# Three quarters of a feed-forward's first product recast in Strassen's form, on an already tuned hybrid block

## The chip, the cores and the metric

One core of a Trainium2 chip runs the whole kernel. The metric is the device time of one execution in microseconds; three executions of the kernel before gave 858.98, 860.34 and 860.87 us, median 860.34 us. One more execution was profiled.

The engines spoken of here are TensorE (PE in the profile, its weight loads PEld), VectorE (DVE), ScalarE (ACT), GpSimd (POOL) and SyncE (SP), which issues most of the DMAs.

## The reference

One layer on 512 frames of 1024 channels. Three gated branches (linear attention, forgetting attention, attention into a memory) are merged and added to the residual; then comes a feed-forward, and a last norm:

```python
u2 = rmsnorm(h, g_ffn[l])
h = h + jnp.square(jax.nn.relu(u2 @ w_ff1[l])) @ w_ff2[l]
return rmsnorm(h, g_final)
```

`w_ff1` is 1024 x 4096 and `w_ff2` 4096 x 1024. The change touches these two products and the last norm. Their inputs and outputs stay float32.

## The kernel before

Every large matmul works on split operands: a float32 block is cast on ScalarE to a high part (fp32r), VectorE subtracts that from the block and so writes the low part, and `mm3` (line 121) issues three matmuls, high by high, high by low, low by high. A weight block is 128 x 1024 (512 KB): SyncE loads it into one of three `raw` tiles of pool `wp`, and its two parts go into one of three `hi`/`lo` pairs. PE's order is written by hand; the order of the other engines' queues comes from a scheduler that runs when the program is built, and each queue is then worked off strictly in that order.

The feed-forward runs in four quarters of 1024 hidden channels (loop at line 1002). In each quarter:

- **First product** (`gT`, line 126): eight blocks of `w_ff1`. One block is eight weight tiles of 128 x 128, each taken by `mm3` against all 512 frames of `u2h`/`u2l`: 24 matmuls with 512 columns. `act_evac` (line 899) applies relu and square on ScalarE and builds seven left factors with VectorE, split into `ch`/`cl`.
- **Second product** (`second`, line 968): Strassen's seven products in Winograd's form, in the order 1, 2, 5, 6, 7, 4, 3. Each takes two weight blocks `i = 0, 1`, twelve 512-column matmuls a block. The right factors 5, 6, 7, 4 are sums of blocks that are formed in place by DMAs of GpSimd that add a second block to the one in SBUF (line 979). `split_b` (line 889) has the three `hi`/`lo` pairs and a fourth of its own (`bhi`/`blo`). Products 1 and 5 stay in PSUM over all quarters (`held`), 6 and 7 are summed in `R6`, `R7`, the others are added to the residual `hN`.

In the last quarter the sums of products 1, 5 and 6 (`E`, `G`) are added to `hN` by six DMAs of GpSimd (line 950), product 7 by VectorE, and `finish` (line 918) norms a row tile as soon as its last half is there and sends both halves out. The first of all tiles, `first`, are computed in halves of 256 frames (`half`, line 855) while the norm of the last frames still runs; `u2_turn` (line 843) transposes the normed frames on PE and splits them into `u2h`/`u2l`.

Below, `c1` to `c14` are the fourteen weight blocks of one second product in PE's order; all fourteen take twelve 512-column matmuls each. `F1` to `F14` are those of the first product in the new form.

Of the kernel before, what the change touches and what calls it, by code (L numbers as in the profile page):

```python
# [17 lines left out]
P = 128  # L18
# [14 lines left out]
def chunk_list():  # L33

    L = []
    L += [("T", "w_mem_kv", P * j) for j in range(4)]
    L += [("N", "w_mem_kv", 2 * j, 512) for j in range(4)]
    L += [("G",)]
    L += [("T", "w_in", OFF["fq"]), ("T", "w_in", OFF["fk"])]
    L += [("N", "w_in", 2 * j, OFF["fv"]) for j in range(4)]  # L40
    for j in range(1, 4):
        L += [("T", "w_in", OFF["fq"] + P * j), ("T", "w_in", OFF["fk"] + P * j)]
    for n, c in (("gk", 2), ("gq", 2)):
        L += [("T", "w_in", OFF[n] + P * j) for j in range(c)]
    L += [("N", "w_in", 2 * j, OFF["gv"]) for j in range(4)]
    for n, c in (("gg", 4), ("mq", 4)):
        L += [("T", "w_in", OFF[n] + P * j) for j in range(c)]
    for g, o in (("gate_fox", "w_fox_o"), ("gate_mem", "w_mem_o"), ("gate_gla", "w_gla_o")):
        for j in range(KT):
            L.append(("T", "w_in", OFF[g] + P * j))  # L50
            if j % 2 == 0:
                L.append(("O", o, j // 2))
    for c in range(2):
        L += [("N", "w_out", 2 * j, 512 * c) for j in range(4)]
    for q in range(4):
        L += [("T", "w_ff1", P * (8 * q + j)) for j in range(8)]
        L += [("B", q, i, b) for b in ("11", "21", "12", "22") for i in range(2)]
    return L
# [3 lines left out]
def hybrid_block(ctx, tc, chunks, wst, xT, memT, xN, cols, gffn, gfin, wup, cst, out):  # L62
# [41 lines left out]

    def load_w(key, eng=None):
        i = index[key]
        raw = wp.tile([P, 1024], F32, tag="raw", name=nm("raw"))
        (eng or nc.sync).dma_start(raw, wst[i])
        return raw

    def split_w(raw):
        hi = wp.tile([P, 1024], F32R, tag="hi", name=nm("whi"))
        lo = wp.tile([P, 1024], F32R, tag="lo", name=nm("wlo"))
        nc.scalar.copy(hi, raw)  # L114
        nc.vector.tensor_tensor(lo, raw, f(hi), op=ALU.subtract)  # L115
        return hi, lo
# [690 lines left out]
    u2h = up.tile([P, KT, S], F32R, tag="uhi", name="u2h")  # L807
    u2l = up.tile([P, KT, S], F32R, tag="ulo", name="u2l")
    with pool("outp") as op_:
# [4 lines left out]
        run(branch("gate_gla", "w_gla_o", ogh, ogl, 2, last=(mh, ml)))  # L814

# [28 lines left out]
        def u2_turn(t):  # L844
            for g in range(2):
# [3 lines left out]
                sl = slice(t * P, (t + 1) * P)  # L849
                last = split(u2h[:, 4 * g:4 * g + 4, sl], u2l[:, 4 * g:4 * g + 4, sl], pt)  # L850
# [4 lines left out]
        def half(j, i, ks=range(KT)):  # L855
            sl = slice(256 * i, 256 * i + 256)
            for k in ks:
                mm3(first[j][:, sl], ws[j][0][:, k, :], ws[j][1][:, k, :], u2h[:, k, sl], u2l[:, k, sl], k == 0, k == KT - 1)
# [12 lines left out]
    mst.close()  # L871
# [7 lines left out]

    with pool("ff") as yp:  # L880
        R6, R7 = ([yp.tile([P, 512], F32, name=f"R{n}{t}") for t in range(2)] for n in (6, 7))
        NQ = 4
        held = {}
        split_n = [0]

        def scratch():
            return yp.tile([P, S], F32, tag="sq", name=nm("sq"), bufs=3)

        def split_b(raw):
            split_n[0] += 1  # L890
# [4 lines left out]
            return [t.rearrange("p (k c) -> p k c", k=2) for t in (hi, lo)]  # L895

        A = []

        def act_evac(ps):

            sq = scratch()
            nc.scalar.activation(sq, ps, AF.Relu)
            nc.scalar.activation(sq, sq, AF.Square)
            if not A or A[-1][2] is not None:
                h, l = (yp.tile([P, 7, 256], F32R, tag=g, name=nm(g), bufs=4) for g in ("ch", "cl"))
                split(h[:, 0, :], l[:, 0, :], sq[:, :256])
                A.append([h, l, None, sq])
                return
            h, l, _, sa = A[-1]
            A[-1][2] = sq  # L910
            split(h[:, 1:3, :], l[:, 1:3, :], sq.rearrange("p (a t) -> p a t", a=2))
            ss = yp.tile([P, 4, 256], F32, tag="ss", name=nm("ss"))
            a11, a21, a12, a22 = sa[:, :256], sa[:, 256:], sq[:, :256], sq[:, 256:]
            for o, x, y in ((0, a21, a22), (2, a11, a21), (1, a11, ss[:, 0, :]), (3, a12, ss[:, 1, :])):
                nc.vector.tensor_tensor(ss[:, o, :], x, y, op=ALU.subtract)
            split(h[:, 3:7, :], l[:, 3:7, :], ss)

        def finish(t, c, n):
            sumsq(scratch(), hN[t], t, c, n)
            if n == 1:  # L920
                r = rms_tile(yp, t)
                for g, eng in ((0, nc.scalar), (1, nc.sync)):
                    gs_ = slice(512 * g, 512 * g + 512)
                    nc.vector.scalar_tensor_tensor(hN[t][:, gs_], hN[t][:, gs_], r, gl[:, gs_], op0=ALU.mult, op1=ALU.mult)
                    eng.dma_start(out[t * P:(t + 1) * P, gs_], hN[t][:, gs_])
# [4 lines left out]
        def add(to, x, op=ALU.add):  # L930
            nc.vector.tensor_tensor(to, to, x, op=op)

        def evac(q, n, t, ps):
            last = q == NQ - 1
            if n == 1 and last:
                add(C(0, 0, t), ps)
            if n in (6, 7):
# [5 lines left out]
            if n == 6 and last:  # L943
                if t == 0:
                    held["G"] = yp.tile([P, 2, 512], F32, tag="ss", name=nm("G"))
                E, G = R6[t], held["G"][:, t, :]
                nc.vector.tensor_tensor(E, held[1][t], R6[t], op=ALU.subtract)
                nc.vector.tensor_tensor(G, held[5][t], E, op=ALU.subtract)
                for to, x in ((C(1, 0, t), E), (C(1, 1, t), G), (C(0, 1, t), G)):
                    nc.gpsimd.dma_start(to, x, accum_op=ALU.add)  # L950
            if n == 7 and last:
                add(C(1, 1, t), R7[t], ALU.subtract)
                finish(2 + t, 1, 0)
                add(C(1, 0, t), R7[t])
# [4 lines left out]
            if n == 3:  # L959
                add(C(0, 1, t), ps)  # L960
                if last:
                    finish(t, 1, 1)
            if n == 2:
                add(C(0, 0, t), ps)
                if last:
                    finish(t, 0, 0)

        def second(q):
            raw = {(b, i): yp.tile([P, 1024], F32, tag=f"b{b}{i}", name=nm("raw")) for b in ("11", "21", "12", "22")
                   for i in range(2)}  # L970
            for (b, i), t in raw.items():
                nc.sync.dma_start(t, wst[index["B", q, i, b]])

            def factor(n, i):

                to, x = {1: ("11", None), 5: ("11", "12"), 6: ("11", "22"), 7: ("12", "22"), 4: ("11", "21"), 3: ("22", None),
                         2: ("21", None)}[n]
                if x is not None:
                    nc.gpsimd.dma_start(raw[to, i], wst[index["B", q, i, x]], accum_op=ALU.add)  # L979
                return split_b(raw[to, i])  # L980

            for n, slot in ((1, 0), (2, 1), (5, 3), (6, 4), (7, 5), (4, 2), (3, 6)):
# [5 lines left out]
                end = q == NQ - 1 and n == 3  # L988
                steps = [[0, 1]] if end else [[0], [1]]
                for js in steps:  # L990
                    w = {i: factor(n, i) for i in js}
                    for t in range(2):
                        for i in js:
                            for k in range(2):
                                p = 2 * i + k
                                sl = slice(t * P, (t + 1) * P)
                                mm3(ps[t], A[p][0][:, slot, sl], A[p][1][:, slot, sl], w[i][0][:, k, :], w[i][1][:, k, :],
                                    p == 0 and not (keep and q), p == 3 and (not keep or q == NQ - 1))
# [3 lines left out]
        for q in range(NQ):  # L1002
            A.clear()
            for j in range(8):
                if q == 0 and j < 2:
                    act_evac(first[j])
                    continue
                key = ("T", "w_ff1", P * (8 * q + j))
                if q == 0 and j < 4:
                    with tc.issue_after(norm_end):  # L1010
                        w = get_w(key)
                else:
                    w = get_w(key)
                run(gT(w, u2h, u2l, act_evac))
# [3 lines left out]
            second(q)  # L1018


def layout(inputs):
# [7 lines left out]
    for i, c in enumerate(chunks):  # L1029
# [4 lines left out]
        elif c[0] == "B":  # L1034
# [3 lines left out]
            for n in range(2):  # L1038
                wst[i, :, 512 * n:512 * n + 512] = W["w_ff2"][(j + 2 * n) * P:(j + 2 * n + 1) * P, cs]
        elif c[0] == "O":  # L1040
# [61 lines left out]
```

## Time and profile before

| | us |
|---|---|
| median of three executions | 860.34 |
| the profiled execution, whole | 859.26 |
| its span, first to last instruction of the program | 857.1 |
| TensorE busy | 840.5 |
| VectorE busy | 498.4 |
| ScalarE busy | 404.3 |
| GpSimd busy | 87.4 |
| stage before the feed-forward tiles (start of `half`) | 0 to 520.2 |
| feed-forward, to the last matmul | 520.2 to 848.3 |

The profile counts a matmul as busy from its start to a modelled end. Matmuls overlap in the array, so what one costs on PE is read from the distance of two starts in the timeline, not from its duration. The same holds, in small, for VectorE and ScalarE: a row that merges several instructions shows their time together.

### The profile page before, as it was taken

Reading aid. Unit: us, or ns where it says so; the run is one execution under the profiler, and the core shown is the slowest. Engines: PE = TensorE matmul, PEld = TensorE weight load, DVE = VectorE, ACT = ScalarE, POOL = GpSimd, SP = SyncE. Lnnn points to the kernel's source line nnn. Section 1 sums busy time; section 2 is a strip of 40 time slices with the busy share of each in tenths; the row PEclk is TensorE's granted clock in tenths of the full one; section 3 lists DMA queues with packets and bytes.
Section 4 is the critical chain, followed back from the end, with each engine's and each line's share of the span. In section 5 each row is a group of like instructions: output and inputs, shape, how many; then the busy total and the mean of one; then the engine's idle time right before and its main releaser. Section 6 shows DMA issues by size and latency. Waiting matters only on the chain.

```text
span 857.1 us, 10630 instructions
## 1 busy us (share of the span) xinstructions
PE 840.5 (98%) x4041; PEld 695.4 (81%) x4041; DVE 498.4 (58%) x832; ACT 404.3 (47%) x646; POOL 87.4 (10%) x96
## 2 busy tenths in 40 slices
PE   8899999999999999999999999999999999999995
PEld 5778788888888888787888889888888888888884
DVE  5775657766444556574533546665556645665577
ACT  8764747754332431322332434655455345535642
POOL 5100000000000011211112100011001000110022
PEclk9999999999999999999999999999999999999998
DMA  8433232322222122124222413969435933791156
GB/s 319 151 123 125 106 115 99 123 75 75 76 96 99 53 96 75 50 74 172 99 98 99 172 50 124 318 122 238 155 97 122 273 123 83 149 281 53 26 102 168
DMA packets 32146, 108.28 MB, mean 126 GB/s; under 512 B 3872, under 2 KB 4832, under 8 KB 32096
## 3 DMA queue, kind: packets, MB, share of 16 engines
q1 hardware_dynamic: 24832, 84.00, 27.3%
q0 software_dynamic: 5472, 18.35, 12.2%
q10 hardware_dynamic: 1792, 5.26, 1.8%
q8 instruction: 32, 0.52, 0.2%
q14 instruction: 18, 0.15, 0.1%
HBM read 103.90 MB, written 2.13 MB: 124 GB/s over the span
## 4 chain that ended last, share of the span: by engine, by line
PE 90%; ACT 3%; DVE 3%; DMA 1%; issue 1%; POOL 0%; SPq 0%; DVEq 0%; POOLq 0%; ACTq 0%
PE mm L122 25%; PE mm L123 24%; PE mm L124 24%; PE a L123 3%; PE a L124 3%; PE a L122 3%; PE a L739 1%; DMA h<-G 1%; PE a L756 1%; PE a L499 1%; PE a L498 1%; PE a L750 1%; DMA memr<-in_memT_dram 1%; PE a L467 1%; PE a L466 1%
## 5 line engine op out<-in xcount | busy, mean ns | idle before, releaser
L115 DVE TENSOR_TENSOR wlo<-raw,whi 128x1024 fp32r<-128x1024 f32 x103 | 129.9, 1264 | 133.4 <-ACT whi L114 131.7
L114 ACT CAST whi<-raw 128x1024 fp32r<-128x1024 f32 x103 | 108.4, 1053 | 168.6 <-PE mm L123 128.4
L122 PE MATMUL mm<-uhi,whi 128*128 128x512 f32 x352 | 139.7, 397 | 0.0
L124 PE MATMUL mm<-uhi,wlo 128*128 128x512 f32 x352 | 137.6, 391 | 0.0
L123 PE MATMUL mm<-ulo,whi 128*128 128x512 f32 x352 | 137.5, 391 | 0.0
L122 PE MATMUL mm<-u2h,whi 128*128 128x512 f32 x240 | 93.4, 389 | 0.0
L123 PE MATMUL mm<-u2l,whi 128*128 128x512 f32 x240 | 93.4, 389 | 0.0
L124 PE MATMUL mm<-u2h,wlo 128*128 128x512 f32 x240 | 93.4, 389 | 0.0
L175 DVE TENSOR_TENSOR lo<-raw,hi 128x1024 fp32r<-128x1024 f32 x42 | 51.2, 1224 | 49.6 <-ACT hi L174 49.1
L124 PEld LDWEIGHTS mm<-uhi,wlo 128*128 128x128 f32 x352 | 66.2, 188 | 14.2
L122 PEld LDWEIGHTS mm<-uhi,whi 128*128 128x128 f32 x352 | 66.4, 189 | 13.5 <-issue 0.7
L123 PEld LDWEIGHTS mm<-ulo,whi 128*128 128x128 f32 x352 | 66.3, 188 | 12.9
L174 ACT CAST hi<-raw 128x1024 fp32r<-128x1024 f32 x42 | 44.0, 1053 | 62.5 <-PE mm L123 23.5
L979 POOL DMA_DIRECT2D raw<-in_wst_dram x32 | 28.1, 877 | 277.2 <-DVE lo L175 208.0
L123 PEld LDWEIGHTS mm<-u2l,whi 128*128 128x128 f32 x240 | 45.0, 188 | 9.4
L122 PEld LDWEIGHTS mm<-u2h,whi 128*128 128x128 f32 x240 | 45.0, 188 | 9.3
L124 PEld LDWEIGHTS mm<-u2h,wlo 128*128 128x128 f32 x240 | 45.0, 188 | 9.3
L122 PE MATMUL mm<-hi,ch 128*128 128x512 f32 x120 | 46.7, 389 | 0.0
L123 PE MATMUL mm<-lo,ch 128*128 128x512 f32 x120 | 46.7, 389 | 0.0
L124 PE MATMUL mm<-hi,cl 128*128 128x512 f32 x120 | 46.7, 389 | 0.0
L590 POOL TENSOR_TENSOR acc<-acc,th 128x512 f32<-128x512 f32 x16 | 24.0, 1503 | 102.7 <-DVE th L589 102.7
L668 POOL MEMSET qpos<- 64x512 f32 x2 | 1.0, 524 | 268.6 <-PE mm L124 268.6
(320 smaller groups left out, 1641.1 us busy)
## 6 DMA issues: line engine op xcount, KB each, us to landing
raw<-in_wst_dram SPq DMA_DIRECT2D x144, 512.0 KB
raw<-in_wst_dram POOLq DMA_DIRECT2D x32, 512.0 KB, 5.3
nFb<-dF ACTq DMA_DIRECT2D x8, 512.0 KB
xr<-in_xT_dram SPq DMA_DIRECT2D x4, 512.0 KB
h<-in_xN_dram SPq DMA_DIRECT2D x4, 512.0 KB
memr<-in_memT_dram SPq DMA_DIRECT2D x4, 256.0 KB
h<-G POOLq DMA_DIRECT2D x4, 256.0 KB, 5.7
out_dram<-h ACTq DMA_DIRECT2D x4, 256.0 KB
```

The source lines that it names most:

```text
L114: nc.scalar.copy(hi, raw)
L115: nc.vector.tensor_tensor(lo, raw, f(hi), op=ALU.subtract)
L122: nc.tensor.matmul(ps, lh, rh, start=start, stop=False)
L123: nc.tensor.matmul(ps, lh, rl, start=False, stop=False)
L124: nc.tensor.matmul(ps, ll, rh, start=False, stop=stop)
L174: nc.scalar.copy(hi, src)
L175: return nc.vector.tensor_tensor(lo, src, f(hi), op=ALU.subtract).ins
L466: nc.tensor.matmul(ps[:, :w], q, K[e][:, 0, :w], start=True, stop=False)
L467: nc.tensor.matmul(ps[:, :w], q, K[e][:, 1, :w], start=False, stop=True)
L498: nc.tensor.matmul(po[:, q0:], vv, PTh[:, c0:c0 + w], start=n == 0, stop=False)
L590: nc.gpsimd.tensor_tensor(acc[j], acc[j], th, op=ALU.add)
L979: nc.gpsimd.dma_start(raw[to, i], wst[index["B", q, i, x]], accum_op=ALU.add)
```

## The change

- **Quarters 2 to 4 of the first product** become Strassen products too (`first_product`). `u2` is kept in four slots of 4 x 256 columns (two halves of the channels by two halves of the frames), with three more slots for sums of them (`u2s`), made on VectorE after the first quarter's fourth tile (`u2_sums`), and one slot overwritten by a sum when the first quarter's tiles are done (`u2_last`). Each half quarter is seven products, in the order 1, 2, 5, 6, 3, 7, 4; each takes one weight block as eight weight tiles against 256 columns. So the weight blocks of a quarter's first product go from 8 to 14, and the matmuls from 192 of 512 columns to 336 of 256. The results are combined by VectorE (`first_evac`).
- **Four of the seven right factors** there are sums of blocks of `w_ff1`. They are made during the earlier stages in DRAM: 24 DMAs of GpSimd, 1 MB each, half of them plain copies and half adding (`next_sum`), each waiting for the cast of every second weight block from the ninth on, and most for an earlier one of the chain to land.
- **The second product** runs 1, 2, 5, 3, 6, 7, 4. Its left factors are now made in three slots of `ch`/`cl` that are rewritten while it runs, and a fourth. Its blocks `11` and `12` go to four tiles of their own (`b11`, `b12`; till `u2_sums` they hold an unsplit copy of `u2`, which `u2_turn` writes with eight more copies on ScalarE), `21` and `22` through the ring of `raw` tiles, which has four now. The fourth `hi`/`lo` pair is gone.
- **The last quarter's corrections** are done by VectorE and the six DMAs are gone. `finish` multiplies the first half by the final gain early; at the end VectorE scales one half of a row tile and ScalarE the other.

```diff
+    tsum = {(n, q): dram.tile([2, P, 1024], F32, name=f"T{n}_{q}") for q in range(1, 4) for n in (1, 2, 3, 4)}
+    def sum_ops():
+        for q in range(1, 4):
+            for n, src, add in ((1, "11", 0), (3, "12", 0), (1, "12", 1), (3, "22", 1), (2, 1, 0), (2, "22", 1), (4, 2, 0),
+                                (4, "21", 1)):
...
+    def next_sum(after):
+        chunk_n[0] += 1
+        op = next(sums, None) if chunk_n[0] > 8 and chunk_n[0] % 2 else None
+        if op is not None:
+            to, src, add_ = op
+            if add_:
+                d = nc.gpsimd.dma_start(to, src, accum_op=ALU.add, max_dma_last_dim=8192)
+            else:
+                d = nc.gpsimd.dma_start(to, src)
+            tc.add_manual_dep(d.ins, after.name, mybir.DependencyInfo(mybir.DependencyClass.Sync, mybir.DependencyReason.DATA),
+                              reason="pace")
...
-                last = split(u2h[:, 4 * g:4 * g + 4, sl], u2l[:, 4 * g:4 * g + 4, sl], pt)
+                last = split(*(x[:, 2 * g + t // 2, :, sl] for x in u2), pt)
+                nc.scalar.copy(plain[t // 2, g].rearrange("p (k t) -> p k t", k=4)[:, :, sl], pt)
...
-            own = split_n[0] % 4 == 0
-            hi, lo = ((yp if own else wp).tile([P, 1024], F32R, tag=g, name=nm(g), bufs=1 if own else 3)
-                      for g in (("bhi", "blo") if own else ("hi", "lo")))
+            hi, lo = (wp.tile([P, 1024], F32R, tag=g, name=nm(g)) for g in ("hi", "lo"))
             split(hi, lo, raw)
...
+        def first_evac(n, i, ps):
...
+            if n == 2:
+                nc.vector.tensor_tensor(a11, a21, ps, op=ALU.add)
+                relu2(a11)
+                left(i, 0, a11)
...
+            if n == 4:
+                add(a21, ps)
+                relu2(a21)
+                late_left(i)
+
+        def first_product(q, i):
+            for n in FIRST:
+                if n in (1, 2, 3):
+                    src = wst[index["F", q, i, {1: "11", 2: "21", 3: "22"}[n]]]
+                else:
+                    src = tsum[{5: 1, 6: 2, 7: 3, 4: 4}[n], q][i]
+                wh, wl = (t.rearrange("p (a k c) -> p a k c", a=2, k=4) for t in ring(src))
+                (uh, ul), s = U2[n]
+                ps = mmt([P, 2, 256])
+                for a in range(2):
+                    for k in range(4):
+                        mm3(ps[:, a, :], wh[:, a, k, :], wl[:, a, k, :], uh[:, s, k, :], ul[:, s, k, :], k == 0, k == 3)
+                first_evac(n, i, ps)
...
             if n == 6 and last:
-                if t == 0:
-                    held["G"] = yp.tile([P, 2, 512], F32, tag="ss", name=nm("G"))
-                E, G = R6[t], held["G"][:, t, :]
-                nc.vector.tensor_tensor(E, held[1][t], R6[t], op=ALU.subtract)
-                nc.vector.tensor_tensor(G, held[5][t], E, op=ALU.subtract)
-                for to, x in ((C(1, 0, t), E), (C(1, 1, t), G), (C(0, 1, t), G)):
-                    nc.gpsimd.dma_start(to, x, accum_op=ALU.add)
+                E, G = R6[t], s1[t]
+                sub(E, E, ps)
+                sub(G, held[5][t], E)
+                add(C(0, 1, t), G)
+                finish(t, 1, 1)
+                add(C(1, 1, t), G)
+                add(C(1, 0, t), E)
```

PE, the first product of quarter 2, at the border of its first two weight blocks (`whi`, `hi` and their low parts hold the weights, `mm` is the PSUM tile). Before:

```order
L122 MATMUL mm_5065<-u2h,whi_5061 128x512
L123 MATMUL mm_5065<-u2l,whi_5061 128x512
L124 MATMUL mm_5065<-u2h,wlo_5062 128x512
L122 MATMUL mm_5103<-u2h,whi_5099 128x512
L123 MATMUL mm_5103<-u2l,whi_5099 128x512
L124 MATMUL mm_5103<-u2h,wlo_5100 128x512
```

And in the changed kernel:

```order
L150 MATMUL mm_5123<-u2h,hi_5119 128x256
L151 MATMUL mm_5123<-u2l,hi_5119 128x256
L152 MATMUL mm_5123<-u2h,lo_5120 128x256
L150 MATMUL mm_5155<-u2h,hi_5151 128x256
L151 MATMUL mm_5155<-u2l,hi_5151 128x256
L152 MATMUL mm_5155<-u2h,lo_5152 128x256
```

A block keeps its 24 matmuls; each has half the columns, and there are 14 blocks in the place of 8.

VectorE, the end of the last second product. `R_4521`, `R_4522` are `R6` of the two upper row tiles, `a_` the PSUM tiles held for products 1 and 5, `lo_` low parts of weight blocks. Before, around the sums of product 6:

```order
L175 TENSOR_TENSOR lo_6796<-raw_6569,hi_6795 128x1024
L931 TENSOR_TENSOR R_4521<-R_4521,mm_6695 128x512
L931 TENSOR_TENSOR R_4522<-R_4522,mm_6696 128x512
L947 TENSOR_TENSOR R_4521<-a_4803,R_4521 128x512
L947 TENSOR_TENSOR R_4522<-a_4804,R_4522 128x512
L175 TENSOR_TENSOR lo_6813<-raw_6570,hi_6812 128x1024
L948 TENSOR_TENSOR G_6726<-a_4873,R_4521 128x512
L948 TENSOR_TENSOR G_6726<-a_4874,R_4522 128x512
```

In the changed kernel at the same place (`R_4582`, `R_4583` are `R6`, `s_` the tiles that take `G`, `h_3638` to `h_3641` the four row tiles of `hN`, `lo_7447` and `lo_7452` the low parts of the last two blocks, c13 and c14):

```order
L929 TENSOR_TENSOR R_4583<-R_4583,mm_7330 128x512
L929 TENSOR_TENSOR s_4576<-a_4923,R_4582 128x512
L932 TENSOR_TENSOR h_3640<-h_3640,R_4582 128x512
L929 TENSOR_TENSOR s_4577<-a_4924,R_4583 128x512
L932 TENSOR_TENSOR h_3641<-h_3641,R_4583 128x512
L203 TENSOR_TENSOR lo_7447<-b_4086,hi_7446 128x1024
L932 TENSOR_TENSOR h_3638<-h_3638,s_4576 128x512
L932 TENSOR_TENSOR h_3640<-h_3640,s_4576 128x512
L932 TENSOR_TENSOR h_3639<-h_3639,s_4577 128x512
L932 TENSOR_TENSOR h_3641<-h_3641,s_4577 128x512
L203 TENSOR_TENSOR lo_7452<-b_4087,hi_7451 128x1024
```

Product 6 is now the third from the end, and six additions to `hN` stand between its result and the low part of the last block.

ScalarE, the transposes ahead of the feed-forward (`a_` are the transposed frames in PSUM, `whi` casts of weight blocks, `hsq` the sum of squares that the norm of the last 128 frames waits for). Before:

```order
L174 CAST u2h<-a_4364 128x4x128
L114 CAST whi_4584<-raw_4582 128x1024
L114 CAST whi_4627<-raw_4625 128x1024
L174 CAST u2h<-a_4390 128x4x128
L796 ACTIVATE hsq_4381,hss_3606<-h_3605 128x512
```

In the changed kernel:

```order
L202 CAST u2h<-a_4413 128x4x128
L141 CAST whi_4630<-raw_4628 128x1024
L883 COPY b_4086<-a_4405 128x4x128
L883 COPY b_4087<-a_4413 128x4x128
L141 CAST whi_4689<-raw_4687 128x1024
L202 CAST u2h<-a_4440 128x4x128
L824 ACTIVATE hsq_4431,hss_3642<-h_3641 128x512
```

Two of the eight copies now stand ahead of that sum.

More of the change, by code (lines that the diff above doesn't have):

```diff
@@ L805, in rms_tile @@
         return r
-    u2h = up.tile([P, KT, S], F32R, tag="uhi", name="u2h")
-    u2l = up.tile([P, KT, S], F32R, tag="ulo", name="u2l")
+    u2 = [up.tile([P, 4, 4, 256], F32R, tag=g, name=n) for g, n in (("uhi", "u2h"), ("ulo", "u2l"))]
     with pool("outp") as op_:
@@ L904, in act_evac @@
[L904 to L913, printed above, removed]
@@ L958, in evac, with load_blocks, factor, second_product @@
                     finish(2 + t, 0, 1)
[L959 to L982, printed above, removed]
+        LEFT = {1: 0, 2: 1, 5: 2, 3: 0, 6: 3, 7: 1, 4: 2}
+        def load_blocks(q):
+            for b, to in (("11", b11), ("12", b12)):
+                for i in range(2):
+                    nc.sync.dma_start(to[i], wst[index["B", q, i, b]])
+        def factor(q, n, i):
+            if n in (2, 3):
+                return ring(wst[index["B", q, i, {2: "21", 3: "22"}[n]]])
+            to, x = {1: (b11, None), 5: (b11, "12"), 6: (b11, "22"), 7: (b12, "22"), 4: (b11, "21")}[n]
+            if x is not None:
+                nc.gpsimd.dma_start(to[i], wst[index["B", q, i, x]], accum_op=ALU.add)
+            return split_b(to[i])
+        def second_product(q):
+            for n in SECOND:
                 keep = n in (1, 5)
```

200 lines of the change are left out of this document (152 added, 48 removed).

## The prediction

> **What bounds the kernel.** I read the page first, then the busy time by stage, then TensorE's timeline.
>
> ```profile
> span 857.1 us, 10630 instructions
> ...
> PE 840.5 (98%) x4041; PEld 695.4 (81%) x4041; DVE 498.4 (58%) x832; ACT 404.3 (47%) x646; POOL 87.4 (10%) x96
> ...
> PE 90%; ACT 3%; DVE 3%; DMA 1%; issue 1%; POOL 0%; SPq 0%; DVEq 0%; POOLq 0%; ACTq 0%
> ```
>
> TensorE holds nine tenths of the chain that ended last. The stretches below are the first and second product of quarter 2 and of quarter 4 (columns: length, then busy time and count for each engine, granted clock, DMA share, GB/s).
>
> ```profile
> 603.36:646.88 43.52, 43.52 (x194) 36.04 (x192) 22.74 (x33) 22.97 (x33) 0.87 (x1) 1.00 0.40 118
> 646.88:684.96 38.08, 38.08 (x170) 31.53 (x168) 24.99 (x28) 17.42 (x18) 5.23 (x6) 1.00 0.80 207
> 766.56:810.08 43.52, 43.52 (x194) 36.04 (x192) 22.74 (x33) 22.97 (x33) 0.87 (x1) 1.00 0.25 70
> 810.08:848.16 38.08, 38.08 (x169) 31.34 (x167) 29.35 (x43) 18.27 (x27) 10.45 (x12) 1.00 0.58 99
> ```
>
> PE is busy all the time at the full granted clock (1.00), and equal stages take equal times: there is no waiting to win back, only matmul time. VectorE, the next engine, fills 52 to 77%.
>
> **Term 1, the matmuls.** The price of one is the distance of starts.
>
> ```profile
> 603.36 0.39 PE L122 MATMUL mm<-u2h,whi 128*128 128x512 f32 x1
> ...
> 646.88 0.39 PE L122 MATMUL a<-hi,ch 128*128 128x512 f32 x1
> ```
>
> 192 matmuls of 512 columns lie between these rows: 43.52 / 192 = 0.2267 us. The halves of the first tiles have exactly the new form, u2 as moving operand in 256 columns:
>
> ```profile
> 525.55 0.28 PE L123 MATMUL mm<-u2l,fhi 128*128 128x256 f32 x1
> ...
> 532.49 0.28 PE L124 MATMUL mm<-u2h,flo 128*128 128x256 f32 x1
> ```
>
> 58 steps lie between these two: 6.94 / 58 = 0.120 us. Half the columns cost 53% of the time, not 50%, and this eats part of what Strassen saves: a quarter's first product goes from 43.52 to 336 x 0.120 = 40.3 us, less by 3.2, and three quarters by **9.6 us**. The second product keeps 168 matmuls of 512 columns, 38.08 us; its new order costs PE nothing.
>
> The Trainium skill, page "TensorE: Matmul & The Clock Gate", section "Back-to-back issue gap", gives N / 2.4 GHz + 2.5 ns, an estimate of 0.216 and 0.109 us; by it the three quarters would save 3 x (192 x 0.2158 - 336 x 0.1092) = 14.2 us. The trace disagrees on both widths, 0.227 and 0.120, in the very kernel, so the measurement decides.
>
> **Term 2, does VectorE keep up?** Its rates, and ScalarE's, from merged rows:
>
> ```profile
> 525.80 1.29 DVE L175 TENSOR_TENSOR u2l<-a,u2h 128x512 fp32r<-128x512 f32 x2 [1.57 <-ACT u2h L174]
> 527.01 3.49 DVE L115 TENSOR_TENSOR wlo<-raw,whi 128x1024 fp32r<-128x1024 f32 x3
> 517.06 1.07 ACT L174 CAST u2h<-a 128x512 fp32r<-128x512 f32 x2 [2.61 <-PE a L848]
> 518.20 1.06 ACT L114 CAST whi<-raw 128x1024 fp32r<-128x1024 f32 x1
> ```
>
> So 0.60 us for each further 512-wide VectorE row (one alone 0.69), 1.15 for a 1024-wide one, on ScalarE 0.5 and about 1.0. In the changed order of VectorE, a first product of quarters 2 and 3 holds 14 low parts and 22 rows of 512: 14 x 1.15 + 22 x 0.60 = 29.3 of 40.3 us (73%). A second product holds 14 and 24: 30.5 of 38.1 us (80%). Both fit. What must also fit is the lead: with three pairs, the cast of a block waits until PE leaves the block three back, two blocks before its own turn: 5.8 us in the first product, 5.4 in the second. Cast and low part take 1.06 + 1.23 = 2.3, so 3.1 to 3.5 us remain for queueing. Walking the queues with these rates, rows that wait for a PE result (the sums of `first_evac`) hold up the next low part by 2 us at most. I take **0** for quarters 2 and 3; bounds 0 to 7, below.
>
> Quarter 4 does not fit so well. Let its second product start at 0; c13 is wanted at 12 x 2.72 = 32.6 and c14, which PE reaches after six matmuls of c13, at 34.0. From the low part of c1 to that of c14 VectorE has 14 x 1.15 + 36 x 0.60 + 0.3 = 38.0 us of rows. It can begin at -4.7 (the block three back ends at -5.8, the cast takes 1.06), so it would be done at 33.3 if it never waited, and it must wait: at 0 for the last result of the first product, and for product 6, whose second tile ends with c10 at 27.2. Behind that stand five rows, the low part of c13, four rows, the low part of c14: 9 x 0.60 + 2 x 1.15 = 7.7, so c14 is ready at about 35.2; my walk through the whole queue, which finds c5 to c8 just in time or 0.1 to 0.5 late, gives 35.8. PE then runs six matmuls of c14 and the twelve of the lower row tile, 1.36 + 2.72, and ends at 39.4 to 40.0 in the place of 38.1.
>
> **The end.** Before:
>
> ```profile
> 847.93 0.39 PE L124 MATMUL mm<-bhi,cl 128*128 128x512 f32 x1
> ...
> 849.66 0.67 DVE L931 TENSOR_TENSOR h<-h,mm 128x512 f32<-128x512 f32 x1
> 850.42 0.63 ACT L796 ACTIVATE sq<-h 128x512 f32<-128x512 f32 x1 [1.32 <-DVE h L931]
> 850.47 1.42 DVE L924 SCALAR_TENSOR_TENSOR h<-h,rr,gl 128x512 f32<-128x512 f32 x2
> 851.80 0.21 DVE L803 TENSOR_SCALAR ms<-hss 128x1 f32<-128x1 f32 x1
> 852.73 1.41 DVE L924 SCALAR_TENSOR_TENSOR h<-h,rr,gl 128x512 f32<-128x512 f32 x2 [0.73 <-POOL rr L804]
> ```
>
> From the last addition (849.66) to the end of the last product with the gain (852.73 + 1.41 = 854.14) pass 4.48 us, then 2.96 to the end of the span. Two things go: the mean no longer stands behind the two products of the tile before (851.80 in the place of about 851.2, 0.6 us), and VectorE does one half, not two (0.7). So 3.2 + 2.96 from the last addition. But in the new queue 13 rows stand between the low part of c14 and that addition, about 6.2 us: it starts at 35.5 + 6.2 = 41.7, later than PE's end asks. End of the span at 41.7 + 6.2 = 47.9 after the start of the second product, before 857.1 - 810.08 = 47.0: **+0.9 us** for stop and tail together. If VectorE never lagged, the addition would start 0.2 after PE's end and the stage would take 38.5 + 6.2 = 44.7: -2.3. If its rows ran 10% slower than the best rate, +3.8 more: +4.7. I take +0.9, the walk, since the rates come from the same forms.
>
> **Smaller edits.** Eight more copies on ScalarE around the transposes:
>
> ```profile
> 519.56 1.05 ACT L114 CAST whi<-raw 128x1024 fp32r<-128x1024 f32 x1 [0.31 <-PE mm L124]
> 520.99 0.63 ACT L796 ACTIVATE hsq<-h 128x512 f32<-128x512 f32 x1
> 522.83 1.41 DVE L826 SCALAR_TENSOR_TENSOR un<-h,rr,gf 128x512 f32<-128x512 f32 x2
> 524.55 1.03 PE L848 MATMUL a<-cst_s,un 128*128 128x128 f32 x8
> ```
>
> Two stand ahead of `hsq`, 1.0 us, of which an idle 0.3 us of ScalarE absorbs a part. `un` ends at 524.24, the transposes start at 524.55 and need its second half 0.4 later: I take **+0.3**, bounds 0 to 1.0. `u2_sums` puts 3 x 2.3 + 1.2 = 8.1 us on VectorE between the low parts of the fourth and fifth tile; three blocks of 5.44 us cover it, and without that cover it would cost the excess over 11 us. `u2_last` waits on ScalarE for half of the last tile, with c1 and c2 already cast ahead of it: nothing. The wait that the second product's sums by DMA impose is eased by the order: 5 and 6 now have product 3 between them, so 10.9 us pass from the one's first block to the other's, for a landing of 5.3 (below).
>
> ```profile
> ACT whi L114 <- PE mm L123: 128.4, 57, 9.3
> ...
> ACT whi L114 <- DMA raw<-in_wst_dram: 5.0, 3, 1.7
> SPq L108 <- DVE wlo L115: 411.8, 76, 15.0
> raw<-in_wst_dram POOLq DMA_DIRECT2D x32, 512.0 KB, 5.3
> 67.72 1.05 ACT L114 CAST whi<-raw 128x1024 fp32r<-128x1024 f32 x1
> 383.28 1.04 ACT L114 CAST whi<-raw 128x1024 fp32r<-128x1024 f32 x1 [1.01 <-PE mm L123]
> 68.00:384.00 316.00, 315.40 (x1612) 263.36 (x1611) 184.43 (x397) 141.70 (x265) 13.88 (x17) 1.00 0.26 89
> ```
>
> The casts that set the pace of the 24 sums in DRAM, the 9th and the 55th, stand at 67.72 and 383.28, so a sum comes every 13 us or so. DMA is busy 26% there. An adding DMA of 512 KB lands in 5.3 us, so one of 1 MB by proportion in 10.6, if DRAM as target costs the same, which no row shows. Casts wait for PE 57 times and for a load only 3: loads come some 14 us early (three blocks of 5.44 less the 2.3 of a split). That lead is the cover; I take **0**, bounds 0 and the rival below. The Trainium skill, "DMA: Bandwidth & Descriptors", section "SWDGE vs HWDGE vs iDMA", says that each DMA engine takes turns between the queues of GpSimd's and of SyncE's DMAs; by that a sum would slow a weight load and not hold it. No run here shows it yet.
>
> **Sum.** Against the profiled execution: 859.26 - 9.6 + 0.9 + 0.3 = 850.9. That execution lies 1.08 below the median of the three runs, so **852.0 us** for the median.
>
> **Rivals.**
> - *VectorE binds in every quarter.* If in-order waits eat the 3 us of lead, each of the other five half quarters loses what the last loses, 1.3 each: 852.0 + 6.5 = 858.5. For: one pair fewer, 80% load. Against: before, the second product of quarter 4 ran with 77% and no gap. Chance 0.15, split over the 0.2% line (1.7 us, about what a measurement of this kernel can tell from no change).
> - *The sums in DRAM starve the weights* (slower). Place: 68 to 384 us. It decides from the point where one adding DMA holds up loads for more than the 14 us of lead, 1.3 times the 10.6 above. At 16 us, twelve of them cost 12 x 2 = 24 us: about 876; GpSimd's small norm steps queue behind some of them and would add to it. Chance 0.12.
> - *VectorE never lags*, -2.3 in the place of +0.9, or matmuls run nearer to the page's gap: 848.8, by the page's gap 847.4. Chance 0.05, of the page's gap 0.02 in it, since 0.120 is measured.
> - *No gain*: the trace's 0.120 holds only for a short stretch, and 256 columns cost 0.1295 when kept up, which makes 336 of them cost 43.5: 861.5. Against: 58 steps in a row were even. Chance 0.03.
>
> My forecast has 0.65. Faster 0.65 + 0.05 + 0.08 = 0.78, same 0.07 + 0.03 = 0.10, slower 0.12. Range 848.0 to 858.5: from the case without lag to VectorE as the bound.
>
> **What would show it.** 128x256 matmuls on `u2h` with starts 0.120 apart and a first product of 40.3 us confirm term 1. Idle PE before c13 or c14 of the last product, released by a low part, confirms term 2; idle PE in quarters 2 and 3 there speaks for the first rival. Casts between 68 and 384 us that wait for `raw` speak for the second. The forecast is wrong if PE shows gaps of over 2 us in any earlier stage.

## The result, and the profile after

| | before | changed |
|---|---|---|
| median of six executions, us | 860.25 | 855.07 |
| lowest and highest | 858.98, 860.87 | 851.76, 857.17 |
| profiled execution, and its span | 859.26, 857.1 | 854.40, 852.6 |

The ratio is 0.9943, 95% interval 0.9927 to 0.9958: faster by 0.6%. The time lies inside the range, and 3 us above the number. The page of the changed kernel, its head, the engines, the chain that ended last, and among the DMA issues the twelve adding ones of the sums in DRAM (their landing, 8.4 us, is the last number):

```profile
span 852.6 us, 11738 instructions
...
PE 831.8 (98%) x4473; PEld 708.0 (83%) x4473; DVE 554.9 (65%) x886; ACT 438.9 (51%) x703; POOL 97.3 (11%) x114
...
PE 86%; DVE 6%; ACT 3%; DMA 3%; issue 2%; SPq 0%; POOL 0%; POOLq 0%; ACTq 0%; DVEq 0%
...
T<-in_wst_dram POOLq DMA_DIRECT2D x12, 1024.0 KB, 8.4
```

PE is busy 8.7 us less and still bounds the kernel; the chain has 4% less of PE, and 3% more of VectorE and 2% more of DMA. The busy time by stage says which stages: first and second product of quarter 2, first product of quarter 4, then its second product up to PE's last row, then the tail.

```profile
605.87:646.18 40.31, 40.31 (x338) 40.31 (x336) 32.29 (x39) 28.02 (x38) 0.86 (x1) 1.00 0.57 199
646.18:684.29 38.11, 38.11 (x171) 31.55 (x169) 30.18 (x37) 20.14 (x24) 6.04 (x7) 1.00 0.86 203
762.71:803.02 40.31, 40.31 (x338) 40.31 (x336) 33.40 (x41) 28.02 (x38) 0.86 (x1) 1.00 0.61 204
803.02:842.88 39.86, 38.93 (x170) 31.13 (x168) 38.50 (x58) 24.26 (x38) 5.42 (x7) 1.00 0.43 79
842.88:852.63 9.75, 0.00 (x1) 0.00 (x0) 3.98 (x9) 2.89 (x6) 1.53 (x2) 0.76 0.49 188
```

A first product takes 40.31 us where it took 43.52, PE without a pause. The last second product takes 39.86 instead of 38.24 with VectorE busy for 38.50 of them, and the tail 9.75 instead of 8.8. So the feed-forward and its end won 9.63 and lost 2.57. But u2's first matmul, at 520.15 us before, now starts at 522.66: 2.5 us were lost ahead of the feed-forward, where the sum has no more than +0.3 for the copies of u2 and 0 for the sums in DRAM. In spans 857.12 - 9.63 + 2.57 + 2.51 = 852.57, and 852.63 was measured.

**Where the 2.5 us went.** TensorE's timeline shows one long pause, at 98 us in the attention stage. The chain of waits, in order of time, leads from it back to a load (columns: start, us, what):

```profile
75.68 2.67 DMA dF<-nF
...
78.87 9.44 DMA nFb<-dF
...
88.55 0.55 DVE nFb L483
89.09 0.60 DVE V L203
89.70 2.27 DVE wlo L142 x2
91.97 0.61 DVE tq L463
...
98.19 2.30 ACT Pt L500 x8
...
101.05 0.87 PE a L510 x2
```

`nFb` is a row of the decay table `dF` broadcast to 128 partitions (512 KB), two of them loaded at once by ScalarE's queue, for the scores of the first two heads. In the timeline of the changed kernel a copy for the sums is issued between the two:

```profile
78.49 0.84 ACTq L480 DMA_DIRECT2D nFb<-dF  x2
78.62 0.50 POOL L128 DMA_DIRECT2D T<-in_wst_dram  x1 [9.10 <-ACT whi L141]
...
88.34 0.76 DVE L483 TENSOR_TENSOR nFb<-nFb,cst_s 128x128 f32<-128x128 f32 x2 [3.99 <-DMA nFb<-dF]
```

Before, the same pair of rows stood 5.5 us apart:

```profile
77.86 0.84 ACTq L452 DMA_DIRECT2D nFb<-dF  x2
...
83.35 0.75 DVE L455 TENSOR_TENSOR nFb<-nFb,cst_s 128x128 f32<-128x128 f32 x2
```

VectorE stands 3.99 us at the second table; the low part of `V`, two weight low parts and `tq` are queued behind it, ScalarE's `Q` waits for `tq`, the softmax for that, PE for the softmax.

The DMA view of the changed kernel, queue by queue, for 79.4 to 82.7, 82.7 to 84 and 84 to 88 us (packets that start in the stretch, MB, share of the 16 DMA engines; q0 carries GpSimd's DMAs, q10 ScalarE's, q1 SyncE's):

```profile
q0 software_dynamic: 16, 1.05, 77.5%
q10 hardware_dynamic: 144, 0.52, 59.7%
...
DMA packets 0, 0.00 MB, mean 0 GB/s; under 512 B 0, under 2 KB 0, under 8 KB 0
...
q1 hardware_dynamic: 144, 0.52, 33.5%
q10 hardware_dynamic: 144, 0.52, 32.0%
```

The copy's megabyte is 16 packets of 64 KB, one for each engine, of 2.6 us each (77.5% of 3.3 us); a table is 144 packets of under 4 KB. By 82.7 us the first table has started all its packets and the copy holds every engine; for 1.3 us no packet of any queue starts; then the second table shares the engines with a weight load.

My theory: the sums in DRAM slow these loads. Rivals: another part of the change costs it (the copies of u2), or sums cost wherever they run.

**Where the end lost 2.57.** The timeline of all engines in the last product of the changed kernel:

```profile
837.42 1.22 DVE L203 TENSOR_TENSOR lo<-b,hi 128x1024 fp32r<-128x1024 f32 x1
...
838.69 0.50 PE L151 MATMUL mm<-lo,ch 128*128 128x512 f32 x1 [0.93 <-DVE lo L203]
...
842.49 0.39 PE L152 MATMUL mm<-hi,cl 128*128 128x512 f32 x1
...
844.43 0.68 DVE L932 TENSOR_TENSOR h<-h,mm 128x512 f32<-128x512 f32 x1
...
846.19 0.98 POOL L832 TENSOR_TENSOR rr<-ms,cst_s 128x1 f32<-128x1 f32 x1 [0.33 <-DVE ms L831]
847.21 0.75 DVE L1057 SCALAR_TENSOR_TENSOR h<-h,rr,gl 128x512 f32<-128x512 f32 x1 [0.44 <-POOL rr L832]
...
847.96 0.37 ACTq L1060 DMA_DIRECT2D out_dram<-h  x1
```

PE waits for the low part of c14 until 838.69; the last addition starts at 844.43, 1.6 us after PE's last row has ended, because VectorE's queue is full; the last product ends at 847.97. From there to the end of the span pass 4.66 us, where 2.97 passed before. Of that the trace shows two things. The last two transfers start together, 0.03 us apart, and land 2.8 us after the last product (before 2.1, in turn). And GpSimd's closing drain instruction ends after them: 4.66 us behind GpSimd's last row, before 3.19. VectorE's queue, the drain, or both?

### The profile page after: what moved, and what is told of

It reads as the page before. It is cut to its first block, busy times and chain, and to the rows that moved or that the text cites. A ratio compares the mean times of both kernels' runs of the same rounds, so it can differ in the third digit from the quotient of the medians.

```text
span 852.6 us, 11738 instructions
## 1 busy us (share of the span) xinstructions
PE 831.8 (98%) x4473; PEld 708.0 (83%) x4473; DVE 554.9 (65%) x886; ACT 438.9 (51%) x703; POOL 97.3 (11%) x114
## 4 chain that ended last, share of the span: by engine, by line
PE 86%; DVE 6%; ACT 3%; DMA 3%; issue 2%; SPq 0%; POOL 0%; POOLq 0%; ACTq 0%; DVEq 0%
PE mm L150 23%; PE mm L151 23%; PE mm L152 23%; PE a L151 3%; PE a L150 3%; PE a L152 3%; DMA nFb<-dF 1%; DVE h L932 1%; PE a L767 1%; DVE lo L203 1%; DMA raw<-in_wst_dram 1%; PE a L784 1%; DMA memr<-in_memT_dram 1%; PE a L527 1%; PE a L526 1%
## 5 line engine op out<-in xcount | busy, mean ns | idle before, releaser
L142 DVE TENSOR_TENSOR wlo<-raw,whi 128x1024 fp32r<-128x1024 f32 x79 | 100.5, 1276 | 99.0 <-ACT whi L141 98.3
L203 DVE TENSOR_TENSOR lo<-b,hi 128x1024 fp32r<-128x1024 f32 x40 | 48.8, 1222 | 26.0 <-ACT hi L202 26.0
L202 ACT CAST hi<-b 128x1024 fp32r<-128x1024 f32 x40 | 41.9, 1048 | 44.5 <-PE mm L152 30.4
L1114 POOL DMA_DIRECT2D b<-in_wst_dram x32 | 27.6, 864 | 273.8 <-DVE lo L203 230.0
L152 PE MATMUL mm<-u2h,lo 128*128 128x256 f32 x192 | 54.3, 283 | 0.0
L151 PE MATMUL mm<-u2l,hi 128*128 128x256 f32 x192 | 54.3, 283 | 0.0
L150 PE MATMUL mm<-u2h,hi 128*128 128x256 f32 x192 | 54.3, 283 | 0.0
L150 PE MATMUL mm<-u2sh,hi 128*128 128x256 f32 x144 | 40.8, 283 | 0.0
L151 PE MATMUL mm<-u2sl,hi 128*128 128x256 f32 x144 | 40.8, 283 | 0.0
L152 PE MATMUL mm<-u2sh,lo 128*128 128x256 f32 x144 | 40.8, 283 | 0.0
```

What stands on the lines that cost most here:

```text
L150: nc.tensor.matmul(ps, lh, rh, start=start, stop=False)
L151: nc.tensor.matmul(ps, lh, rl, start=False, stop=False)
L152: nc.tensor.matmul(ps, ll, rh, start=False, stop=stop)
L202: nc.scalar.copy(hi, src)
L203: return nc.vector.tensor_tensor(lo, src, f(hi), op=ALU.subtract).ins
L1114: nc.gpsimd.dma_start(to[i], wst[index["B", q, i, x]], accum_op=ALU.add)
```

## The experiments

`tail_left_out`, `tail_e_dma` and `copies_act` build on `sums_from_25`, `best` joins the last two, `best_gain` adds to it. The traces' numbers side by side (own: the profiled execution; PE lost: starts further apart than their price, 70 to 130 us; last addition and PE done: us from the start of the last second product; DMAs: issued by GpSimd in the whole program; drain: from GpSimd's last row to the drain's end):

```
kernel           own  PE lost  last addition  PE done  last product to end  DMAs  drain
before        859.26     2.88          39.58    38.24                 2.97    38   3.19
after         854.40     5.92          41.41    39.86                 4.66    56   4.66
sums_from_25  851.94     2.87          41.41    39.82                 4.66    56   4.66
sums_from_13  853.00     2.88          41.41    39.82                 4.66    56   4.66
sums_even     852.86     4.23          41.41    39.83                 4.66    56   4.66
before_sums   866.87     8.63          39.79    38.24                 4.48    62   5.15
tail_gpsimd   859.05     7.79          42.94    41.33                 4.66    56   4.66
tail_left_out 850.00     2.89          39.01    38.60                 4.66    56   4.66
tail_e_dma    851.34     2.88          40.20    38.63                 4.82    58   4.82
copies_act    851.36     2.88          41.41    39.82                 3.80    44   3.68
best          849.86     2.88          40.21    38.64                 3.84    46   3.85
best_gain     851.77     2.88          39.01    38.63                 4.49    46   3.84
```

### The sums moved in time

```diff
-        op = next(sums, None) if chunk_n[0] > 8 and chunk_n[0] % 2 else None
+        op = next(sums, None) if chunk_n[0] > 24 and chunk_n[0] % 2 else None
```

> The changed kernel with one number moved: the first sum in DRAM is issued at the 25th weight cast (about 179 us), no longer at the 9th (67 us), the last at the 71st (483 us). Theory (the 1 MB copy issued at 78.6 us makes the broadcast loads of nFb land 9.4 us after their issue, and VectorE, ScalarE and then PE stand behind them): PE's gaps between 98 and 104 us fall back from 3.9 to about 1.3 us, u2's first matmul comes 2.3 to 2.5 us earlier, and the time falls by 2.3 us, to about 852.7 (ratio to the kernel before 0.991). Rival (the 2.5 us ahead of the feed-forward product come from something else, such as the eight copies or more code): no change, 855. Second rival (sums cost wherever they run): as much is lost later, after 179 us, as is won at 98.

Median 851.85 (851.53 to 852.45), ratio 0.9908, interval 0.9896 to 0.9921. PE's loss is back at the value of before, u2 starts at 520.22, and nothing is lost later. The theory holds, both rivals fall: the loss comes with the sums' place and not with their number or with the eight copies. The spread shrank from 5.4 us to 0.9 with it.

The same line with `> 12`:

> The changed kernel with the first sum at the 13th cast (about 88 us), so that only the two copies at 68.8 and 78.6 us leave the place of the first two nFb loads; the other six loads still share the DMA engines with a sum now and then. Theory: those two copies are the whole loss, so as with a start at the 25th, about 852.7 us and nFb landing in 5 us or less at 83 us. Rival (each sum near any nFb load costs): a part of the 2.3 us stays, 853.5 to 855.

852.5 (851.85 to 853.5), ratio 0.9915, interval 0.9900 to 0.9929: as expected. The other six `nFb` loads do no harm, although sums run beside them: the one issued at 122.78 us has VectorE's addition 7.9 us after its issue, where before it took 4.3 (121.52 to 125.80), and PE's loss is 2.88 as before. Those loads have slack, the first two have none.

The same line with `> 8` and `chunk_n[0] % 2 == 0`:

> The changed kernel with the sums at the even casts from the 10th on, not at the odd ones from the 9th: the same 24 sums at the same distance, one cast later, so that the first copies are issued at about 73 and 84 us, on either side of the first two nFb loads (78.5 us), and none right at them. Theory (what costs is the one copy that is issued together with the first nFb loads): nFb lands by about 84.5, PE's gaps from 98 to 108 us come to 1.3 to 2, the time to about 852.5. Rival (any sum in DRAM in the attention stage costs, whatever its phase): about 855 as with the change.

853.43 (852.29 to 854.29), interval 0.9909 to 0.9939: between the two, so the theory was too narrow. The pair is late although no copy is issued with it:

```profile
79.36 0.86 ACTq L480 DMA_DIRECT2D nFb<-dF  x2
...
84.36 0.50 POOL L128 DMA_DIRECT2D T<-in_wst_dram  x1 [10.77 <-ACT whi L141]
...
86.49 0.76 DVE L483 TENSOR_TENSOR nFb<-nFb,cst_s 128x128 f32<-128x128 f32 x2 [4.32 <-DMA nFb<-dF]
...
87.77 0.75 DVE L483 TENSOR_TENSOR nFb<-nFb,cst_s 128x128 f32<-128x128 f32 x2
```

The second table's addition comes 8.4 us after the issue, between the 5.5 of before and the 9.9 of the change. What shares the engines with the pair is not a sum but weight loads. The DMA view for 74 to 78.7 us, while the copy issued at 72.86 runs, and for 80.5 to 85.5, while the pair loads:

```profile
q0 software_dynamic: 32, 1.05, 67.9%
q1 hardware_dynamic: 50, 0.02, 3.3%
...
q10 hardware_dynamic: 220, 0.82, 49.7%
q1 hardware_dynamic: 156, 0.54, 33.5%
```

SyncE issued a weight load at 74.37 us, and next to nothing of it moves until the copy is done; before, the load issued at 74.84 was through by 77.8, ahead of the pair. By these times the copy cost the pair through a load that it had put off; the copy at 84.36 sends nothing before 85.5. It is a matter of degree: what is in flight while the pair loads.

### The sums alone in the kernel before

```diff
-        nc.scalar.copy(hi, raw)
+        cast = nc.scalar.copy(hi, raw)
         nc.vector.tensor_tensor(lo, raw, f(hi), op=ALU.subtract)
+        next_sum(cast.ins)
```

> The kernel before with the 24 sums in DRAM alone, paced as in the change (blocks of the second product's weights are summed, and nobody reads the sums). Theory (the sums cost 2.3 us through the nFb loads, and nothing else): 862.5 us, ratio 1.0027, with PE gaps of about 3.7 us between 97 and 103 us in the place of 1.3. Rival (the sums are free): 860.2, ratio 1.000. Rival of the prediction (sums starve the weights): over 865.

Eleven executions gave 860.43 to 866.87, median 861.47, ratio 1.0032, interval 1.0017 to 1.0048. The direction is as expected, but the sums cost in two ways that the expectation had not parted: six of the runs lie between 860.4 and 861.5, about what GpSimd's longer drain gives (the end grew by 4.48 - 2.97 = 1.5), and five lie 1 to 5 us above them. No trace of the six was kept, so the drain as their whole cost is not shown. The profiled execution is the worst, and shows why a late table is so dear. Windows just before and after PE's pause, granted clock third from the end of a row; first the kernel before, then the changed one, then this one:

```profile
98.00:103.00 5.00, 4.41 (x23) 3.21 (x22) 3.73 (x11) 4.92 (x10) 0.00 (x0) 1.00 0.46 182
103.00:109.00 6.00, 6.00 (x31) 5.04 (x30) 5.22 (x19) 3.95 (x11) 0.00 (x0) 1.00 0.35 122
```

```profile
98.00:103.00 5.00, 2.88 (x13) 2.05 (x12) 3.33 (x13) 4.87 (x13) 0.00 (x0) 0.75 0.75 288
103.00:109.00 6.00, 6.00 (x28) 5.03 (x28) 4.64 (x13) 4.22 (x10) 0.83 (x1) 0.92 0.17 25
```

```profile
98.00:103.00 5.00, 1.05 (x6) 0.60 (x4) 3.53 (x12) 4.92 (x12) 0.00 (x0) 0.85 0.69 243
103.00:109.00 6.00, 5.91 (x20) 4.64 (x20) 3.79 (x9) 4.21 (x7) 0.00 (x0) 0.55 0.16 66
```

The clock in these rows is a mean over the window. After a pause of 4 us it is 0.55 for the next six, with PE busy and a third fewer matmuls done; after one of 2.0 it fell too (0.50 from 102 to 103 us, 1.00 again from 104), after one of 1.6 (`sums_even`) it stayed at 1.00 in both windows. In this run the second table's addition starts 11.4 us after the issue. So a pair that is 2.9, 4.4 and 5.9 us later than before (8.4, 9.9 and 11.4 against 5.5) costs PE 1.4, 3.0 and 5.8 us: first there is some slack, then the clock adds to it. A fourth trace, `tail_gpsimd` below, has the sums of the change and a pair 4.6 us late; its pause is 2.8 us, the clock is 0.50 from 102 to 108 us, and PE loses 4.9. So the price is not in proportion to the delay, and it differs from run to run of the same sums.

### The end

```diff
-                nc.vector.tensor_tensor(h[c], h[c], g_[c], op=ALU.mult)
+                nc.gpsimd.tensor_tensor(h[c], h[c], g_[c], op=ALU.mult)
...
-                add(C(1, 1, t), G)
-                add(C(1, 0, t), E)
+                nc.gpsimd.tensor_tensor(C(1, 1, t), C(1, 1, t), G, op=ALU.add)
+                nc.gpsimd.tensor_tensor(C(1, 0, t), C(1, 0, t), E, op=ALU.add)
```

> The changed kernel with eight 512-wide rows of the last quarter moved from VectorE to GpSimd: the additions of E and G to the lower row of blocks (four) and the four products with the gain that do not end the kernel. Theory (VectorE's queue, with no idle time from 829 us on, sets when the last addition starts): the low part of c14 comes 2.4 us earlier, PE's stop of 1.1 us goes, the last addition starts about 39 us after the last second product, not 41.4, and the stage falls from 49.6 to about 47.2; time 852.6. Rival (the end is set by the landing of the last transfers and GpSimd's drain, 4.6 us after the last product, or GpSimd's rows slow VectorE): under 0.5 us won, 854.6 or more.

856.72 (855.4 to 859.05), interval 0.9956 to 0.9981: no gain, and the last addition 1.5 us later. The timeline of VectorE shows a low part that took 2.00 us and two additions that took 3.47, where the changed kernel's low part took 1.22 and four additions of this form 2.49:

```profile
836.50 2.00 DVE L203 TENSOR_TENSOR lo<-b,hi 128x1024 fp32r<-128x1024 f32 x1
838.42 3.47 DVE L932 TENSOR_TENSOR h<-h,s 128x512 f32<-128x512 f32 x2
...
844.39 1.27 DVE L932 TENSOR_TENSOR h<-h,mm 128x512 f32<-128x512 f32 x2
```

In the same times on GpSimd:

```profile
837.38 3.97 POOL L1090 TENSOR_TENSOR h<-h,s 128x512 f32<-128x512 f32 x2
...
844.52 1.29 POOL L1054 TENSOR_TENSOR h<-h,gl 128x512 f32<-128x512 f32 x1 [3.18 <-DVE ms L831]
```

Where VectorE reads two operands from SBUF, both engines are slow; at 844.4, where one operand is PSUM (`mm`), both run at their usual pace. The Trainium skill, "SBUF — State Buffer", section "SBUF: two separate sides", says so: the two engines take one port pair by an exclusive lock, for a VectorE instruction with two SBUF inputs among others; the trace agrees, by 3.47 for two of the additions against 2.49 for four. It does not tell VectorE's queue from the drain, so the rows were taken away without another engine's help:

```diff
-                add(C(1, 1, t), G)
-                add(C(1, 0, t), E)
```

> sums_from_25 without the four additions of E and G to the lower row of blocks (so the lower 256 rows of the output lack a part of the product). Theory (VectorE's queue sets the end): the low part of c14 comes 2.4 us earlier, PE's stop of 1.09 us goes, the last addition starts 39.0 us after the last second product instead of 41.4, and the span and time fall by 2.4, to about 849.5. Rival (landing of the last transfers and GpSimd's drain set the end): the stop goes, the time falls by 0.5 at most.

850.04 (849.96 to 851.8), interval 0.9875 to 0.9905. Last addition at 39.01, PE done at 38.60, the stage 47.20 us instead of 49.60: VectorE's queue sets the end, and each row of 0.6 us in it counts in full. From last product to end stays 4.66: that part has another cause.

```diff
+                nc.gpsimd.dma_start(C(1, 0, t), E, accum_op=ALU.add)
                 add(C(1, 1, t), G)
-                add(C(1, 0, t), E)
```

> sums_from_25 with the two additions of E to the lower row of blocks done by two adding DMAs of GpSimd, as the kernel before did them, no longer by VectorE. Theory (VectorE's queue sets the end): two rows of 0.6 us less ahead of c14, the last addition 1.2 earlier, two further DMAs in GpSimd's drain: about 850.8. Rival (the additions land too late, 6 us after E is there, and VectorE stands at product 7's addition): no gain, 851.5 to 852.5.

The trace does what the theory says: last addition at 40.20, PE done at 38.63, drain 4.82 with 58 DMAs, stage 48.56 instead of 49.60. The time, 851.6 (850.48 to 853.62), interval 0.9888 to 0.9924, cannot tell 1 us from none in four runs.

```diff
-                d = nc.gpsimd.dma_start(to, src)
+                d = nc.scalar.dma_start(to, src)
```

> sums_from_25 with the 12 plain copies of the sums issued by ScalarE's DMA queue in the place of GpSimd's, so that GpSimd issues 44 DMAs in all and not 56. Theory (GpSimd's drain at the end takes 0.082 us for each DMA that it issued in the whole program: 3.19 us after its last row with 38 of them, 4.66 with 56, 5.15 with 62): 3.68 us from its last row to the end of its drain, SyncE's last wait is then the later one, and the time falls by 0.6, to about 851.2. Rival (the length of the drain comes from something else): 4.66 us again and no change in time.

The drain took 3.68 us as expected, and the span ends 3.80 after the last product and no longer 4.66. Time 851.43 (851.18 to 851.71), interval 0.9885 to 0.9918; the step of 0.4 in the medians is within the spread, the trace's 0.86 is not. The drain follows 0.09 + 0.0817 x (DMAs that GpSimd issued) through all six counts, 38 to 62.

### All repairs together

> The three repairs together: sums from the 25th cast on, the 12 plain copies by ScalarE's DMA queue, the two additions of E by GpSimd DMAs. If they add up: the last addition 40.2 us after the last second product starts, 46 DMAs in GpSimd's drain (3.85 us), the last stage 47.7 us, time 851.85 - 1.0 - 0.8 = 850.0 (ratio 0.989). Rival (they overlap: with the last addition earlier, the landing of the last transfers ends the span): 850.6 to 851.2.

849.92 (849.8 to 853.3), ratio 0.9897, interval 0.9879 to 0.9914; the stage takes 47.58. They add up, and this version beats both kernels.

```diff
+                x = nc.vector.tensor_tensor(C(1, 0, t), C(1, 0, t), ps, op=ALU.add).ins
...
+                        with tc.issue_after(x):
+                            nc.vector.tensor_tensor(C(1, 1, u), C(1, 1, u), gl[:, 512:], op=ALU.mult)
```

> The same, and of the last two row tiles the product of the upper half with the gain is put behind the last addition (two rows of VectorE, 0.6 us each, out of the queue ahead of it). If VectorE's queue still sets the end: last addition at 39.0, then 0.5 us later to the mean, stage 47.0, time 849.3. Rival (PE's end at 38.6 and the four last transfers, which now start together, take over): as best or up to 0.5 us slower.

850.88 (849.98 to 851.77), interval 0.9879 to 0.9906, stage 47.58 as without it. The last addition starts at 39.01, but the way from there to the last product grew from 3.53 to 4.08, and the four last transfers, now together, take 4.49 to the end: the rival. VectorE's queue stops deciding here.

## Why the prediction was right, and where its number was off

- **Term 1** holds to the digit: 336 x 0.120 was forecast as 40.3, and all three first products took 40.31. A price read from 58 steps held for 336 in a row, so the rival of 0.1295 falls.
- **Quarters 2 and 3 at nothing** holds: in the waits of PE from 603 us on there is one group in all, in the last product. With 30 to 33 us of VectorE's work in 38 to 40, three pairs give enough lead; the rival in which VectorE binds everywhere falls.

```profile
PE mm L151 <- DVE lo L203: 0.9, 1, 0.9
```

- **The walk through quarter 4** holds: c14's low part was forecast for 35.2 to 35.8 and was there at 838.64 - 803.02 = 35.6; the last addition for 41.7 and started at 41.41; PE for 39.4 to 40.0 and ended at 39.86. `tail_left_out` shows that the cause is the one named.
- **The tail was mis-sized**, in "So 3.2 + 2.96 from the last addition": 3.54 + 4.66 were measured, 2.04 more, and the term came to +2.57 in the place of +0.9. The 2.96 was carried over from before as if it were fixed. 0.86 of the difference is the drain (`copies_act`); the next 0.83 goes with the two last transfers that start together, which no run parted from it; 0.34 lies between the addition and the last product (3.54, not 3.2), and its cause is open.
- **The eight copies**, +0.3, cost nothing: `sums_from_25` starts u2 at 520.22, before 520.15.
- **The sums at 0 is the step that failed**, in "That lead is the cover; I take 0". The lead was that of weight loads through SyncE, and it covered those: the waits of ScalarE's weight casts between 68 and 384 us name PE, not `raw`. But the first two `nFb` have no such lead. They are loaded when `dF` is ready and wanted at once, and the trace of before had the wait in a view that the prediction didn't ask, what waits for the tile (us, times; which of the six waits PE stands behind, it doesn't say):

```profile
  DVE nFb L455: 11.2, 6
```

  The price is 855.07 - 851.85 = 3.2 us between medians, 0.9943 - 0.9908 or 3.0 us between ratios, and 854.40 - 851.94 = 2.5 between the two profiled executions. The rival on starved loads named the wrong load and the wrong form: no threshold at 14 us, but a table 4.4 us late. The Trainium skill, "DMA: Bandwidth & Descriptors", section "SWDGE vs HWDGE vs iDMA", has each DMA engine take turns between queues; the trace agrees, and shows that one turn of the copy is a packet of 2.6 us. So "slow a weight load and not hold it" was wrong for that long: while the copy had all the engines, nothing else started. The adding sums, with `max_dma_last_dim=8192`, go in packets of 8 KB (128 of them, from 90.8 to 99 us); no run did the same for the copies.
- **The 1.08 us** between the profiled execution and the median was added as if it belonged to every kernel; `sums_from_25` has 851.94 and 851.85 there. What it was in the kernel before is open. Together 852.0 + 3.2 + 1.7 - 0.3 - 1.1 = 855.5, and 855.07 was measured; the profiled executions have 2.14 us outside the span before and 1.77 after, which no term counts and which is about the size of the rest. That the last two misses run against the first two is luck.

The sentence on what would make the forecast wrong, gaps of over 2 us in an earlier stage, came true at 98 us; the time stayed in the range all the same, whose upper end another rival had set. That is luck too.

## What to carry to other kernels

Work in the background isn't free because the stream that one looked at has lead: list every load that runs in the same time and ask each for its slack, above all those that are issued when they are already wanted. Look at the size of the packets too, not only at the bytes. The end of a program is priced with its own rows: what is queued on the engine that finishes last, which transfers start together, and how many DMAs GpSimd has issued. Moving rows from VectorE to GpSimd won nothing here, because VectorE's rows beside them read both operands from SBUF.

## What the runs showed of the hardware

- GpSimd's closing drain takes 0.082 us for each DMA it has issued in the whole program (3.19, 3.68, 3.85, 4.66, 4.82 and 5.15 us with 38, 44, 46, 56, 58 and 62). Before it hid behind the last transfer; with 56 it ended the program.
- TensorE's clock falls to half after a short pause: to 0.50 (0.75 as the mean of the window) after a pause of 2.0 us with a few scattered transposes behind it, transposes 0.21 us apart and not 0.11, and not after one of 1.6, in one trace each. The Trainium skill, "TensorE: Matmul & The Clock Gate", section "Part 1: The HAM clock gate", gives an idle window of some 3.4 us for that; here less idle time was enough.
- A 1 MB copy in DRAM took each DMA engine for one packet of 64 KB and 2.6 us, in which no packet of another queue started there (the changed kernel from 82.7 to 84 us).
- A 1 MB sum in DRAM landed sooner than the 10.6 us estimated by proportion, the adding ones in 8.4 us (above) and the copies in 5.7, as the view of the DMAs has it (count, median us to landing):

```profile
T<-in_wst_dram POOLq DMA_DIRECT2D x6, 5.7
```
